# RMS normalisation: the inverse root mean square by an add and a power on GpSimd in place of Sqrt on ScalarE and a reciprocal on VectorE

## The chip, the cores and the metric

The kernel runs on one core of a Trainium2 chip. The metric is the device time of one execution in microseconds (us), the median over several executions. The engines are named as in the profile: PE (TensorE), DVE (VectorE), ACT (ScalarE), POOL (GpSimd) and SP (SyncE, which here only issues transfers). Each runs its own instructions in the order in which they were written and waits for others by semaphores.

## The reference

```python
batch, seq, dim = 16, 1024, 512          # x: 16 x 1024 x 512 float32, gamma: ones(512)

def reference(x, gamma):
    eps = 1e-5
    rms = np.sqrt(np.mean(x ** 2, axis=-1, keepdims=True) + eps)
    return (x / rms * gamma).astype(np.float32)
```

There are 16,384 rows of 512 numbers. Each row is divided by its own root mean square and multiplied by gamma, number by number. 33.55 MB are read and as many written.

## The kernel before

**Tiling.** The rows are cut into four tiles t = 0 to 3 of 128 partitions x 32 rows x 512 numbers (8.4 MB each). Three of them fit into the buffers `slot0` to `slot2`; tile 3 goes into slot 0 again, once tile 0 has been stored from there. Compute works in nine groups, `(t, g, n, pieces, share)` in the list `groups`: group (t, g) is the n rows per partition from row g of tile t. The first two groups have 7 and 9 rows, the other seven have 16.

**The work of a group.**
- `square_sums` (L88): for each piece of 7, 5 or 4 rows ACT squares into a scratch buffer (L92), DVE sums along the row into `ss` (L93). `ss` has one column per row of the group.
- `inverse_rms` (L97): ACT takes Sqrt(ss / 512 + eps) of all n columns (L98), DVE the reciprocal (L99). The result stands in `ss` and is called `rstd`.
- `scale_by_pool` (L102): POOL takes the last `share` rows (7 of 16, as a rule; 3 in the last group), multiplies them by `rstd` (L105) and then by gamma (L106), in place.
- `scale` (L111): ACT multiplies the other `mine` rows by `rstd`, one instruction per row (L114); `times_gamma` (L116): DVE multiplies them by gamma in one instruction (L118).

**The order** is written out by hand. Iteration k issues, for group k, `scale_by_pool`; the first two pieces of `square_sums` of group k + 1; the first half of `scale`; the third piece of k + 1; the second half of `scale`; `times_gamma`; the transfers; and at its very end `inverse_rms` of group k + 1. So before the change the Sqrt of group k + 1 stands behind the last L114 of group k on ACT, and its reciprocal behind L118 of group k on DVE. POOL's queue has L105 and L106 of each group and nothing else after the start.

**Transfers.** All are issued by SP, in one queue. `load` is at L45 and `store` at L49. The loads of tiles 0 and 1 are issued at the start and those of tile 2 after the first group, among three one-row stores. After group (0, 16) follow the stores of rows 3 to 15 and 16 to 31 of tile 0 and the two loads of tile 3; tiles 1 and 2 are stored whole, after groups (1, 16) and (2, 16), and tile 3 in halves, after (3, 0) and (3, 16). A store waits on SP for POOL's and DVE's products, and what follows it on SP waits too.

**Start.** Gamma arrives as one row; TensorE multiplies a column of ones with it (L66), which spreads it over 128 partitions of `gamma_psum`, and ACT copies that into `gamma_b` for POOL (L161). L72 is a Sqrt on one column of constants.

Of the kernel before, what the change touches and what calls it, by code (L numbers as in the profile page):

```python
# [9 lines left out]
def kernel(  # L10
# [6 lines left out]
    nc = tc.nc  # L17
    P = nc.NUM_PARTITIONS
    eps = 1e-5
    fp32 = mybir.dt.float32  # L20
    AF = mybir.ActivationFunctionType
    OP = mybir.AluOpType
# [3 lines left out]
    N, D = xf.shape  # L26
# [9 lines left out]
    const = ctx.enter_context(tc.tile_pool(name="const", bufs=1))  # L36
# [24 lines left out]
    load(1, 1, 16, 32)  # L61

    ones_col = const.tile([1, P], fp32)
    nc.gpsimd.memset(ones_col, 1.0)  # L64
    gamma_psum = psum.tile([P, 1, D], fp32, name="gamma_psum")
    nc.tensor.matmul(gamma_psum[:, 0], ones_col, gamma_row, start=True, stop=True)  # L66
    gamma_b = const.tile([P, 1, D], fp32)

    eps_t = const.tile([P, 1], fp32)
    nc.gpsimd.memset(eps_t, eps)  # L70
    table = const.tile([P, 1], fp32)
    nc.scalar.activation(out=table, in_=eps_t, func=AF.Sqrt)  # L72


    groups = [
# [19 lines left out]
        )  # L95

    def inverse_rms(ss, n):  # L97
        nc.scalar.activation(out=ss[:, :n, 0], in_=ss[:, :n, 0], func=AF.Sqrt, bias=eps_t, scale=1.0 / D)  # L98
        nc.vector.reciprocal(out=ss[:, :n, 0], in_=ss[:, :n, 0])  # L99
        return ss  # L100

    def scale_by_pool(rstd, t, g, n, share):  # L102
# [44 lines left out]
    def pieces_of(group):  # L147
        t, g, n, pieces, share = group
        ss = stats.tile([P, 16, 1], fp32, name="ss")
        r = 0  # L150
        todo = []
        for k, m in enumerate(pieces):
            todo.append((ss, t, g, r, m, k))
            r += m
        return ss, todo

    ss, todo = pieces_of(groups[0])
    for piece in todo:
        square_sums(*piece)
    rstd = inverse_rms(ss, groups[0][2])  # L160
    nc.scalar.copy(out=gamma_b[:, 0], in_=gamma_psum[:, 0])  # L161
    for k, group in enumerate(groups):
        t, g, n, pieces, share = group
        mine = n - share
        half = (mine + 1) // 2
        ahead = groups[k + 1 :][:1]
        ss, todo = pieces_of(ahead[0]) if ahead else (None, [])
        scale_by_pool(rstd, t, g, n, share)
        for piece in todo[:2]:
            square_sums(*piece)  # L170
        scale(rstd, t, g, 0, half)
        for piece in todo[2:]:
            square_sums(*piece)
        scale(rstd, t, g, half, mine)
        times_gamma(t, g, 0, mine)
        transfers(t, g)
        for nxt in ahead:
            rstd = inverse_rms(ss, nxt[2])
# [30 lines left out]
```

## Time and profile before

| | |
|---|---|
| median of 3 executions | 161.61 us (161.46 to 161.80) |
| the profiled execution | 161.56 us |
| its span in the profile | 159.5 us |
| DVE, ACT, POOL busy | 112.5, 108.2, 106.4 us (71%, 68%, 67%) |
| read and written | 33.56 and 33.55 MB, 421 GB/s over the span |

The span is what the profiler saw of the program on the core; the time of the execution has 2.06 us around it. A group of instructions is shown as line, engine, operation, output and inputs with their shapes, then the count, the busy time in all, the mean ns of one, and the idle time of the engine just before them with what ended it. The digits of a row of slices are tenths of a fortieth of the span. The transfers have a row of their own, since they run on DMA engines beside the five.

### The profile page before, as it was taken

Reading aid. Unit: us, or ns where it says so; the run is one execution under the profiler, and the core shown is the slowest. Engines: PE = TensorE matmul, PEld = TensorE weight load, DVE = VectorE, ACT = ScalarE, POOL = GpSimd, SP = SyncE. Lnnn points to the kernel's source line nnn. Section 1 sums busy time; section 2 is a strip of 40 time slices with the busy share of each in tenths; the row PEclk is TensorE's granted clock in tenths of the full one; section 3 lists DMA queues with packets and bytes.
Section 4 is the critical chain, followed back from the end, with each engine's and each line's share of the span. In section 5 each row is a group of like instructions: output and inputs, shape, how many; then the busy total and the mean of one; then the engine's idle time right before and its main releaser. Section 6 shows DMA issues by size and latency. Waiting matters only on the chain.

```text
span 159.5 us, 280 instructions
## 1 busy us (share of the span) xinstructions
PE 2.0 (1%) x2; PEld 0.5 (0%) x2; DVE 112.5 (71%) x42; ACT 108.2 (68%) x111; POOL 106.4 (67%) x24
## 2 busy tenths in 40 slices
PE   0050000000000000000000000000000000000000
PEld 0010000000000000000000000000000000000000
DVE  0028597997989999999999999899997019500000
ACT  3072989859999998998999499999942970000000
POOL 1000947986998699999999999999999940000000
DMA  5999999999999999999999999996996996999995
GB/s 199 424 431 493 427 394 419 501 394 394 460 394 396 454 415 419 427 452 403 509 403 394 501 419 394 526 526 263 526 493 296 526 493 296 394 435 485 394 403 255
DMA packets 2747, 67.12 MB, mean 421 GB/s; under 512 B 313, under 2 KB 314, under 8 KB 698
## 3 DMA queue, kind: packets, MB, share of 16 engines
q1 hardware_dynamic: 2746, 67.11, 98.2%
q14 instruction: 1, 0.01, 0.0%
HBM read 33.56 MB, written 33.55 MB: 421 GB/s over the span
## 4 chain that ended last, share of the span: by engine, by line
DMA 38%; DVE 29%; ACT 16%; issue 2%; ACTq 0%; SPq 0%
DMA out_dram<-slot 22%; DMA slot<-in_x_dram 17%; DVE ss L93 17%; DVE slot L118 12%; ACT slot L114 8%; ACT sq_psum L92 6%; ACT sq_sbuf L92 1%; ACTq L204 0%; ACT ss L98 0%; ACT gamma_b L161 0%; DVE ss L99 0%; SPq L49 0%; ACTq L92 0%
## 5 line engine op out<-in xcount | busy, mean ns | idle before, releaser
L105 POOL TENSOR_TENSOR slot<-slot,ss 128x3584 f32<-128x3584 f32 (+2 forms) x9 | 46.9, 5216 | 21.7 <-DVE ss L99 21.7
L93 DVE TENSOR_REDUCE ss<-sq_psum 128x7 f32<-128x3584 f32 (+1 forms) x16 | 49.2, 3073 | 16.5 <-ACT sq_psum L92 16.5
L106 POOL TENSOR_TENSOR slot<-slot,gamma_b 128x3584 f32<-128x3584 f32 (+2 forms) x9 | 59.2, 6582 | 0.7
L114 ACT ACTIVATE slot<-slot,ss 128x512 f32<-128x512 f32 x75 | 47.5, 709 | 4.7 <-DVE ss L99 4.7
L118 DVE TENSOR_TENSOR slot<-slot,gamma_psum 128x4608 f32<-128x4608 f32 (+2 forms) x9 | 41.3, 4592 | 8.5 <-ACT slot L114 8.5
L92 ACT ACTIVATE sq_psum<-slot 128x3584 f32<-128x3584 f32 (+1 forms) x16 | 40.2, 2512 | 8.4 <-DMA slot<-in_x_dram 7.0
L93 DVE TENSOR_REDUCE ss<-sq_sbuf 128x5 f32<-128x2560 f32 x8 | 22.5, 2808 | 0.0
L92 ACT ACTIVATE sq_sbuf<-slot 128x2560 f32<-128x2560 f32 x8 | 18.6, 2323 | 0.0
L98 ACT ACTIVATE ss<-ss,eps_t 128x16 f32<-128x16 f32 (+2 forms) x9 | 2.7, 304 | 8.4 <-DVE ss L93 8.4
L99 DVE RECIPROCAL ss<-ss 128x16 f32<-128x16 f32 (+2 forms) x9 | 2.1, 237 | 0.4 <-ACT ss L98 0.4
L66 PE MATMUL gamma_psum<-gamma_row,ones_col 1*128 1x512 f32 x2 | 2.0, 1120 | 8.6 <-DMA gamma_row<-in_gamma_dram 8.6
L72 ACT ACT_TABLE_LOAD x1 | 1.3, 1283 | 1.1 <-PEq L193 1.1
L161 ACT COPY gamma_b<-gamma_psum 128x512 f32<-128x512 f32 x1 | 0.6, 565 | 0.0
L66 PEld LDWEIGHTS gamma_psum<-gamma_row,ones_col 1*128 1x128 f32 x2 | 0.5, 304 | 8.6 <-issue 8.6
L64 POOL MEMSET ones_col<- 1x128 f32 x1 | 0.2, 195 | 0.3 <-POOLq L193 0.3
L193 POOL MEMSET const-float32-0.0<- 128x1 f32 x1 | 0.1, 99 | 0.2 <-issue 0.2
L72 ACT ACTIVATE table<-eps_t 128x1 f32<-128x1 f32 x1 | 0.2, 202 | 0.0
L193 POOL MEMSET const-bfloat16-1.0<- 128x1 bf16 x1 | 0.1, 103 | 0.0
L193 POOL MEMSET const-uint8-127<- 128x1 uint8 x1 | 0.1, 103 | 0.0
L193 POOL MEMSET const-float32-1.0<- 128x1 f32 x1 | 0.1, 99 | 0.0
L70 POOL MEMSET eps_t<- 128x1 f32 x1 | 0.1, 89 | 0.0
## 6 DMA issues: line engine op xcount, KB each, us to landing
slot<-in_x_dram SPq DMA_DIRECT2D x6, 4096.0 KB, 21.8
out_dram<-slot SPq DMA_DIRECT2D x3, 4096.0 KB, 23.3
slot<-in_x_dram SPq DMA_DIRECT2D x4, 2048.0 KB, 9.9
out_dram<-slot SPq DMA_DIRECT2D x1, 3328.0 KB, 34.5
out_dram<-slot SPq DMA_DIRECT2D x3, 256.0 KB, 31.9
gamma_row<-in_gamma_dram SPq DMA_DIRECT2D x4, 0.4 KB
out_dram<-slot SPq DMA_DIRECT2D x2
gamma_row<-in_gamma_dram SPq DMA_DIRECT2D x1, 0.5 KB
```

Of the source, the lines that this page charges most:

```text
L66: nc.tensor.matmul(gamma_psum[:, 0], ones_col, gamma_row, start=True, stop=True)
L72: nc.scalar.activation(out=table, in_=eps_t, func=AF.Sqrt)
L92: nc.scalar.activation(out=sq[:, :m], in_=rows, func=AF.Square)
L93: nc.vector.tensor_reduce(out=ss[:, r : r + m, 0], in_=sq[:, :m], axis=mybir.AxisListType.X, op=OP.add)
L98: nc.scalar.activation(out=ss[:, :n, 0], in_=ss[:, :n, 0], func=AF.Sqrt, bias=eps_t, scale=1.0 / D)
L99: nc.vector.reciprocal(out=ss[:, :n, 0], in_=ss[:, :n, 0])
L105: nc.gpsimd.tensor_tensor(out=part, in0=part, in1=by_row, op=OP.mult)
L106: last = nc.gpsimd.tensor_tensor(out=part, in0=part, in1=gamma_b.to_broadcast([P, share, D]), op=OP.mult)
L114: nc.scalar.activation(out=x[:, g + r, :], in_=x[:, g + r, :], func=AF.Copy, scale=rstd[:, r])
L118: scaled = nc.vector.tensor_tensor(out=part, in0=part, in1=gamma_psum.to_broadcast([P, r1 - r0, D]), op=OP.mult)
L161: nc.scalar.copy(out=gamma_b[:, 0], in_=gamma_psum[:, 0])
L193: nc = _bacc.Bacc("TRN2", target_bir_lowering=False, num_devices=1)
```

## The change

`inverse_rms` becomes two instructions on POOL: an add of 512 x eps to the sum of squares, and a power with the exponent -0.5, each with its second operand spread from one column. As the sum is not divided by 512 any more, gamma is multiplied by the square root of 512 where it is spread: the column of ones that TensorE multiplies with it becomes a column of that number. The Sqrt at L72 and its constants go; two other constant columns are written on POOL.

```diff
     ones_col = const.tile([1, P], fp32)
-    nc.gpsimd.memset(ones_col, 1.0)
+    nc.gpsimd.memset(ones_col, D**0.5)
...
-    eps_t = const.tile([P, 1], fp32)
-    nc.gpsimd.memset(eps_t, eps)
-    table = const.tile([P, 1], fp32)
-    nc.scalar.activation(out=table, in_=eps_t, func=AF.Sqrt)
+    eps_d = const.tile([P, 1, 1], fp32)
+    nc.gpsimd.memset(eps_d, eps * D)
+    power = const.tile([P, 1, 1], fp32)
+    nc.gpsimd.memset(power, -0.5)
...
     def inverse_rms(ss, n):
-        nc.scalar.activation(out=ss[:, :n, 0], in_=ss[:, :n, 0], func=AF.Sqrt, bias=eps_t, scale=1.0 / D)
-        nc.vector.reciprocal(out=ss[:, :n, 0], in_=ss[:, :n, 0])
+        nc.gpsimd.tensor_tensor(
+            out=ss[:, :n], in0=ss[:, :n], in1=eps_d.to_broadcast([P, n, 1]), op=OP.add
+        )
+        nc.gpsimd.tensor_tensor(
+            out=ss[:, :n], in0=ss[:, :n], in1=power.to_broadcast([P, n, 1]), op=OP.pow
+        )
         return ss
```

The place of `inverse_rms` in the order stays: at the end of iteration k, for group k + 1. On POOL that is behind L106 of group k.

## The prediction

> **What bounds the kernel now.** I read the page's 40 slices and queue table first, since 67 MB moved in 159.5 us suggests transfers. They say that the DMA engines never rest, from slice 2 to the end:
>
> ```profile
> DMA  5999999999999999999999999996996996999995
> q1 hardware_dynamic: 2746, 67.11, 98.2%
> ```
>
> The three 6s have to be checked, so next I cut the span into long stretches (columns: busy us and instructions of PE, its weight load, DVE, ACT and POOL, clock, DMA share, GB/s):
>
> ```profile
> 0.00:2.00 2.00, 0.00 (x0) 0.00 (x0) 0.00 (x0) 0.85 (x1) 0.44 (x6) 1.00 0.30 70
> 72.00:109.00 37.00, 0.00 (x0) 0.00 (x0) 36.10 (x15) 34.07 (x34) 36.77 (x6) 1.00 1.02 439
> 109.00:138.00 29.00, 0.00 (x0) 0.00 (x0) 20.80 (x7) 16.18 (x25) 20.20 (x5) 1.00 1.00 434
> 138.00:158.00 20.00, 0.00 (x0) 0.00 (x0) 0.00 (x0) 0.00 (x0) 0.00 (x0) 1.00 0.97 419
> ```
>
> The share is 1.00 and more from 72 to 138 us, where the 6s lie: a 6 is large packets falling into unequal slices, not a pause. So the transfers set the time, at about 433 GB/s, where a 4096 KB store (4.19 MB) is 9.7 us of data. In 72 to 109 us POOL is busy 36.77 of 37 us and DVE 36.10: the compute engines are full as well, but they run ahead of the transfers. By how much is read from issue and landing (last column: us from issue to landing) of the first load, issued at 0.74, and of the last two stores, issued at 123.16 and 138.0:
>
> ```profile
> slot<-in_x_dram SPq DMA_DIRECT2D x1, 2048.0 KB, 7.2
> out_dram<-slot SPq DMA_DIRECT2D x1, 4096.0 KB, 25.9
> out_dram<-slot SPq DMA_DIRECT2D x1, 4096.0 KB, 20.7
> ```
>
> The stores land at 149.1 and 158.7, 9.6 us apart: the last one only queued. On an empty queue the first load took 7.2 us, of which 2.10 MB / 433 GB/s = 4.8 is data and so 2.3 us other latency; the last store alone would take 9.7 + 2.3 = 12.0. To land at 158.7 it need only be issued at 146.7. **Compute has 8.7 us to spare** (146.7 - 138.0). The chain of waits stops at the last DVE instruction and does not show this.
>
> What sets the 138.0 is in the timeline (start, duration, engine, line):
>
> ```profile
> 109.11 6.17 POOL L105 TENSOR_TENSOR slot<-slot,ss 128x3584 f32<-128x3584 f32 x1
> ...
> 115.36 7.78 POOL L106 TENSOR_TENSOR slot<-slot,gamma_b 128x3584 f32<-128x3584 f32 x1
> ...
> 117.72 0.31 ACT L98 ACTIVATE ss<-ss,eps_t 128x16 f32<-128x16 f32 x1 [0.56 <-DVE ss L93]
> 122.46 0.25 DVE L99 RECIPROCAL ss<-ss 128x16 f32<-128x16 f32 x1
> 122.74 8.07 ACT L114 ACTIVATE slot<-slot,ss 128x512 f32<-128x512 f32 x13 [4.71 <-DVE ss L99]
> 123.09 2.75 POOL L105 TENSOR_TENSOR slot<-slot,ss 128x1536 f32<-128x1536 f32 x1
> ...
> 130.85 7.09 DVE L118 TENSOR_TENSOR slot<-slot,gamma_psum 128x6656 f32<-128x6656 f32 x1 [8.14 <-ACT slot L114]
> ```
>
> POOL starts its pair L105, L106 at 53.12, 67.11, 81.12, 95.10, 109.11 and 123.09: every 14.0 us, with no idle. From the last inverse root mean square (122.71) to the last store are 15.3 us: 8.1 on ACT, 7.1 on DVE, the rest waits.
>
> **What the Trainium skill says.** GPSIMD Engine Reference, 3.1 (side-by-side cycle accounting), gives about 2.6 cycles per element for a two-input elementwise instruction; Specifications gives 1.2 GHz. The trace agrees roughly, by the groups kept apart by shape:
>
> ```profile
> L106 POOL TENSOR_TENSOR slot<-slot,gamma_b 128x3584 f32<-128x3584 f32 x6 | 46.8, 7794 | 0.5
> L105 POOL TENSOR_TENSOR slot<-slot,ss 128x3584 f32<-128x3584 f32 x6 | 37.0, 6164 | 3.9 <-DVE ss L99 3.9
> ...
> L106 POOL TENSOR_TENSOR slot<-slot,gamma_b 128x1536 f32<-128x1536 f32 x2 | 6.9, 3437 | 0.2
> ...
> L105 POOL TENSOR_TENSOR slot<-slot,ss 128x1536 f32<-128x1536 f32 x2 | 5.5, 2751 | 14.7 <-DVE ss L99 14.7
> ```
>
> L105: (6164 - 2751) / 2048 = 1.67 ns, 2.0 cycles; L106: 2.13 ns, 2.6 cycles. Both leave 0.19 us fixed (2751 - 1536 x 1.667). The same page, 7 (performance pitfalls for Q7 kernels), gives 4 cycles for each step of a dependent fp32 chain. No page prices a power. Perfetto Trace Analysis, Tensor Engine Instruction, calls GPSIMD strict FIFO; here every POOL pair runs in program order.
>
> **The change part by part.** Removed: nine Sqrt on ACT (0.30 us) and nine reciprocals on DVE (0.25). That is worth nothing at the end: neither engine ends the kernel while transfers do, and both pace less tightly than POOL (reciprocals at 52.79, 66.48, 80.17: 13.7 us per group). It does bring squares forward by up to 0.5 us, where ACT stood waiting at L98.
>
> The table warm-up at L72 goes; a table load must then stand ahead of the first Square. I cost it at 0: the load takes 1.28 us (ScalarE: Activation LUTs, "What ACT_TABLE_LOAD costs", says about 1283 ns, as the trace does) and the first rows land at 7.9. Without that cover it would be 1.3 us once, early, inside POOL's idle of 3.2 us at 25 us. The memsets of other values cost the same; the second constant is some 0.1 us at 1 us, under the wait for data.
>
> Added: two POOL instructions per group, and a **new place in a queue**. The reciprocal of the next group stood behind L118 on DVE. The add and the power stand behind L106 of this group on POOL, and POOL has no idle there. Behind them wait L105 on POOL, L114 on ACT, L118 on DVE and the store on SP. So each group's period becomes 14.0 + q, with q the add, the power and gaps.
>
> - Add on 128x16: 0.19 + 16 x 1.67 ns = 0.22 us.
> - Gaps: 0.1 us for two more handovers (L105 ends 59.29, L106 starts 59.36: 0.07 each, rounded down).
> - Power on 128x16: unknown. The floor is an add, 0.22 us. The page's Specifications give eight cores with 16 fp32 lanes, so one column of 128 rows is one vector step, 16 per instruction. A power is a logarithm, a product and an exponential, which I take as some 20 to 40 dependent steps with range handling: at 4 cycles 80 to 160 cycles, or 0.07 to 0.13 us a column if columns don't overlap. Overlapped, it could be a third; done lane by lane, 16 times as much (some 20 to 30 us). I take **2.1 us** (0.19 + 16 x 0.12), in the upper half, since a generic loop with special cases seems likelier to me than a pipelined one.
>
> So q = 0.22 + 2.1 + 0.1 = 2.4 us for 16 columns. Sum over the path: the sums of squares of group (0, 16) are ready at 34.9, up to 0.5 sooner by the freed ACT; I take 34.5. POOL is free then: group (0, 7) can begin at 22.7, takes 1.6 for its nine columns and 10.1 for its pair, to 34.4. From there POOL is never idle again: seven q and six pairs of 14.0 to the last inverse root, 34.5 + 84 + 7 x 2.4 = 135.3. With the 15.3 behind it, the last store is issued at 150.6, 3.9 us beyond 146.7. It then starts on an empty queue and is late by all of that. The profiled execution took 161.56 us for a span of 159.5, that is 2.06 around it, and the median is 161.61: 161.6 + 3.9 = **165.5 us**.
>
> The same sum gives the threshold: 34.5 + 84 + 7q + 15.3 = 146.7 at q = 1.84, a power of 1.5 us. Below, nothing shows; above, each further us of power costs 7 us, and 9 once the two short groups queue too. Earlier stores don't decide: that of (2, 16) goes out at 104.5 + 5q and has 38.8 us of data and 3.1 of latency and close behind it, to 146.4 + 5q, less than the last store's 146.6 + 7q.
>
> **The rivals.**
> - **A, forecast: power of 1.5 to 3.5 us.** Ends 161.9 to 177 (3.5 us: the two short groups at q = 2.0 and 2.4, seven at 3.8; POOL from 15.05 on is 100.4 of pairs plus 31.0; 146.5 + 15.3 = 161.8 issue, 15.1 late).
> - **B, not slower: the transfers hide it.** One mechanism: the 8.7 us of room before the last store. It decides for q up to 1.84. POOL even starts ahead, because at 24.8 and 37.0 the inverse root no longer waits behind L118. Time 161.6. For it speaks that an overlapped vector loop needs under 1 us; against it, that seven groups each pay.
> - **C, the power is very slow (over 3.5 us)**, partly or wholly lane by lane. At 5 us: q of 5.3 (seven), 2.6 and 3.2 sum to 42.9; 15.05 + 100.4 + 42.9 + 15.3 = 173.7, plus 12.8 to the end of the span and 2.06: 188.5. At 20 us, over 300.
> - **D, faster**: ACT and DVE relieved. The engines that move data are busy 98.2% of the span, and the rest is the start and the last landing, which the change leaves alone. At most a few tenths: 161.2.
> - That the change doesn't do what it says, as by a table load that waits for data, comes out as B.
>
> **How the numbers follow.** Chances: A 0.40, B 0.37, C 0.18, D 0.05. About 0.2% (0.3 us) is what can be told from no change. A gives slower, C too: 0.58; B gives 0.37 within; D 0.05 faster. The range takes in B and A whole and C to a power of some 4.3 us (183): 161.2 to 183, leaving out some 0.12 of C and a little of D. A alone: 161.9 to 177.
>
> **What would show it.** After: add and power between L106 and the next L105; their mean is the whole question. POOL's pair would start every 14.0 + q from 37 us on. If q is above 1.84, the last store lands some 12 us after its issue and the DMA row has a real gap before it; if below, it lands later than that and the row stays full. I am wrong in mechanism if the DMA row has gaps earlier than the last stores, if POOL is idle between groups, or if L105 or L106 themselves change length.

## The result and the profile after

| | before | after |
|---|---|---|
| median of 4 executions | 161.71 us (161.46 to 163.47) | 171.82 us (171.66 to 171.92) |
| ratio to before | | 1.060, 95% interval 1.0525 to 1.0675 |
| profiled execution, its span | 161.56, 159.5 us | 171.83, 170.0 us |
| POOL, DVE, ACT busy | 106.4, 112.5, 108.2 us | 131.8, 112.0, 105.7 us |

The kernel is slower, as forecast, but by 10.1 us where 3.9 were forecast. The page of after, its DMA row, queue table and chain of waits:

```profile
DMA  5999999999898999999999999997559995950885
q1 hardware_dynamic: 2746, 67.11, 92.4%
POOL 73%; ACT 7%; DVE 6%; DMA 4%; issue 1%; ACTq 0%; POOLq 0%
```

The same 67.11 MB now fill 92.4% of a longer span, and the chain runs 73% over POOL. Before, it was made of DMA, DVE and ACT:

```profile
DMA 38%; DVE 29%; ACT 16%; issue 2%; ACTq 0%; SPq 0%
```

The 5s and the 0 late in the row of after have to be explained. After, cut into stretches around them (columns as before: PE, its weight load, DVE, ACT, POOL, clock, DMA share, GB/s):

```profile
109.00:118.00 9.00, 0.00 (x0) 0.00 (x0) 5.50 (x3) 9.00 (x10) 8.92 (x2) 1.00 1.07 466
118.00:122.00 4.00, 0.00 (x0) 0.00 (x0) 4.00 (x2) 2.69 (x2) 4.00 (x1) 1.00 0.00 0
122.00:151.00 29.00, 0.00 (x0) 0.00 (x0) 12.55 (x5) 15.49 (x23) 26.32 (x9) 1.00 1.01 434
151.00:158.00 7.00, 0.00 (x0) 0.00 (x0) 6.67 (x1) 0.00 (x0) 0.00 (x0) 1.00 0.00 0
158.00:168.00 10.00, 0.00 (x0) 0.00 (x0) 0.00 (x0) 0.00 (x0) 0.00 (x0) 1.00 0.98 419
```

These two are real pauses, but shorter than they look. A packet is booked where it starts, and the large ones take 2.4 us each, so a stretch can show 0.00 while packets that started before it still move. From the start and length of every packet in the trace, none is under way for 3.2 us (119.7 to 122.9) and for 6.4 us (152.2 to 158.6), 9.6 of the 10.5 us by which the span grew. Before, neither existed. The first ends when the store of tile 2 is issued (122.1), the second when the last store is (157.7). The groups of after, kept apart by shape, show what filled POOL:

```profile
L101 POOL TENSOR_TENSOR ss<-ss,power 128x16 f32<-128x16 f32 x7 | 20.3, 2906 | 0.5
...
L101 POOL TENSOR_TENSOR ss<-ss,power 128x9 f32<-128x9 f32 x1 | 1.8, 1797 | 0.1
L98 POOL TENSOR_TENSOR ss<-ss,eps_d 128x16 f32<-128x16 f32 x7 | 1.5, 218 | 0.0
L101 POOL TENSOR_TENSOR ss<-ss,power 128x7 f32<-128x7 f32 x1 | 1.5, 1488 | 0.1
```

The add costs 0.22 us as worked out; the power on 16 columns costs 2.91 us, not 2.1. From 7 to 16 columns it grows by (2906 - 1488) / 9 = 158 ns a column, and 0.38 us is fixed. The end of the timeline of after:

```profile
125.29 6.16 POOL L109 TENSOR_TENSOR slot<-slot,ss 128x3584 f32<-128x3584 f32 x1
...
131.53 7.77 POOL L110 TENSOR_TENSOR slot<-slot,gamma_b 128x3584 f32<-128x3584 f32 x1
...
139.26 0.21 POOL L98 TENSOR_TENSOR ss<-ss,eps_d 128x16 f32<-128x16 f32 x1
139.55 2.91 POOL L101 TENSOR_TENSOR ss<-ss,power 128x16 f32<-128x16 f32 x1
142.49 8.07 ACT L118 ACTIVATE slot<-slot,ss 128x512 f32<-128x512 f32 x13 [9.82 <-POOL ss L101]
...
150.59 7.09 DVE L122 TENSOR_TENSOR slot<-slot,gamma_psum 128x6656 f32<-128x6656 f32 x1 [12.93 <-ACT slot L118]
```

POOL runs L109, L110, add, power without a pause, every 17.27 us (108.01 to 125.29) where the pair alone took 14.0. ACT stands for 9.82 us until the last power is done at 142.46; before, the last reciprocal was done at 122.71. What lies behind it is as long as before (15.2 us to the issue), and the last store landed 11.1 us after its issue: it no longer queued.

### The profile page after: what moved, and what is told of

It reads as the page before. It is cut to its first block, busy times and chain, and to the rows that moved or that the text cites. A ratio compares the mean times of both kernels' runs of the same rounds, so it can differ in the third digit from the quotient of the medians.

```text
span 170.0 us, 290 instructions
## 1 busy us (share of the span) xinstructions
PE 2.0 (1%) x2; PEld 0.5 (0%) x2; DVE 112.0 (66%) x33; ACT 105.7 (62%) x101; POOL 131.8 (78%) x43
## 3 DMA queue, kind: packets, MB, share of 16 engines
q1 hardware_dynamic: 2746, 67.11, 92.4%
## 4 chain that ended last, share of the span: by engine, by line
POOL 73%; ACT 7%; DVE 6%; DMA 4%; issue 1%; ACTq 0%; POOLq 0%
POOL slot L110 33%; POOL slot L109 26%; POOL ss L101 13%; ACT slot L118 4%; DMA slot<-in_x_dram 4%; DVE slot L122 4%; ACT sq_psum L92 3%; DVE ss L93 2%; POOL ss L98 1%; ACTq L208 0%; POOLq L109 0%; POOLq L110 0%
## 5 line engine op out<-in xcount | busy, mean ns | idle before, releaser
L118 ACT ACTIVATE slot<-slot,ss 128x512 f32<-128x512 f32 x75 | 47.5, 707 | 31.4 <-POOL ss L101 31.4
L110 POOL TENSOR_TENSOR slot<-slot,gamma_b 128x3584 f32<-128x3584 f32 (+2 forms) x9 | 59.3, 6585 | 0.7
L92 ACT ACTIVATE sq_psum<-slot 128x3584 f32<-128x3584 f32 (+1 forms) x16 | 40.1, 2505 | 12.3 <-DMA slot<-in_x_dram 6.6
L109 POOL TENSOR_TENSOR slot<-slot,ss 128x3584 f32<-128x3584 f32 (+2 forms) x9 | 46.9, 5215 | 0.7
L101 POOL TENSOR_TENSOR ss<-ss,power 128x16 f32<-128x16 f32 (+2 forms) x9 | 23.6, 2626 | 0.7
L98 POOL TENSOR_TENSOR ss<-ss,eps_d 128x16 f32<-128x16 f32 (+2 forms) x9 | 1.9, 215 | 14.3 <-DVE ss L93 14.3
L72 POOL MEMSET power<- 128x1 f32 x1 | 0.1, 89 | 0.0
```

The lines of the kernel that those rows point to most:

```text
L92: nc.scalar.activation(out=sq[:, :m], in_=rows, func=AF.Square)
L98: nc.gpsimd.tensor_tensor(out=ss[:, :n], in0=ss[:, :n], in1=eps_d.to_broadcast([P, n, 1]), op=OP.add)
L101: nc.gpsimd.tensor_tensor(out=ss[:, :n], in0=ss[:, :n], in1=power.to_broadcast([P, n, 1]), op=OP.pow)
L109: nc.gpsimd.tensor_tensor(out=part, in0=part, in1=by_row, op=OP.mult)
L110: last = nc.gpsimd.tensor_tensor(out=part, in0=part, in1=gamma_b.to_broadcast([P, share, D]), op=OP.mult)
L118: nc.scalar.activation(out=x[:, g + r, :], in_=x[:, g + r, :], func=AF.Copy, scale=rstd[:, r])
```

## The experiments

The theory: POOL's queue sets the pace, because the power stands in it behind L110 with nothing idle; this delays the stores until the transfers run dry, and the last store most, as ACT and DVE do their 15.2 us behind the last power. The rivals: the place alone, or the handovers from POOL to ACT; POOL's busy time alone, wherever it is spent; the other edits (gamma's factor, constants, table).

**Another instruction in the same place (e1).**

```diff
-            out=ss[:, :n], in0=ss[:, :n], in1=power.to_broadcast([P, n, 1]), op=OP.pow
+            out=ss[:, :n], in0=ss[:, :n], in1=power.to_broadcast([P, n, 1]), op=OP.mult
```

> The changed kernel with a multiply in place of the power: same place in POOL's queue, same waits; the power itself is left out. Theory (the length of the power, paid once per group in POOL's queue): the 16-column instruction falls from 2.91 to about 0.22 us, the period of POOL from 17.27 to about 14.6, the last store is issued near 138 us, inside the room before the transfers: 161.6 us. Rival 1 (the place: ACT and DVE now wait for POOL at the end of each group, whatever the instruction takes): most of the 10 us stays, over 168. Rival 2 (the table warm-up or gamma's factor): stays at 171.8.

161.96 us, ratio 1.0006 (0.9995 to 1.0016). The group and the DMA row of e1:

```profile
L101 POOL TENSOR_TENSOR ss<-ss,power 128x16 f32<-128x16 f32 x7 | 1.5, 216 | 0.6
```
```profile
DMA  6999999999999999999999999996996996999993
```

With 0.22 us in the power's place the row has the same three 6s as before the change and no 5: the last store went out at 138.1 us, as it did before. The place, the waits and all other edits are still there, so none of them carries the loss by itself. The place is not free: POOL starts a group every 14.57 us (93.71 to 108.28) instead of 14.0. But its first large group starts 2.0 us sooner than before (35.41 for 37.36), since its inverse root no longer stands behind L118 on DVE, and so the last inverse root is done at 122.77, where it was done at 122.71 before.

**Half of the columns (e2).**

```diff
+        m = 8 if n == 16 else n
-            out=ss[:, :n], in0=ss[:, :n], in1=power.to_broadcast([P, n, 1]), op=OP.pow
+            out=ss[:, :m], in0=ss[:, :m], in1=power.to_broadcast([P, m, 1]), op=OP.pow
```

> The changed kernel with the power on 8 of the 16 columns in the seven large groups; for the other 8 the power is left out. By the three widths in the trace of after (7: 1.49, 9: 1.80, 16: 2.91 us) 8 columns take 1.65 us. Theory (period, then a threshold): period 16.0, last power ends at 35.6 + 6 x 16.0 + 1.95 = 133.6, last store issued at 148.9, about 2 us past the latest issue that the transfers hide (146.7 to 147.3): 163.2 to 163.8. Rival (every microsecond of the power counts, no room before the last store): 171.8 - 7 x 1.26 = 163.0, so this run alone doesn't tell it; with e1 at 161.6 and not at 153 it does.

162.50 us, ratio 1.0045 (1.0031 to 1.006): above before, and 0.7 us under the lower end of what was expected. The power and the last two stores of e2 (groups by shape; then issue and landing):

```profile
L102 POOL TENSOR_TENSOR ss<-ss,power 128x8 f32<-128x8 f32 x7 | 11.5, 1645 | 0.5
```
```profile
out_dram<-slot SPq DMA_DIRECT2D x1, 4096.0 KB, 18.1
```
```profile
out_dram<-slot SPq DMA_DIRECT2D x1, 4096.0 KB, 11.1
```

Eight columns took the 1.65 us of the straight line. The store before the last was issued at 131.2 and landed at 149.3; the last was issued at 148.4 and landed after 11.1, as on the empty queue of after. So this is the edge: the transfers had just about run dry (by the packets' times, for 0.2 us). It gives the room before the last store better than the first load did. From issue to the end of the span are 11.9 us (148.4 to 160.3), so the latest issue that costs nothing is 159.5 - 11.9 = 147.6, not 146.7, or 148.2 if the 0.2 us without a packet are taken off 148.4: the room is 9.6 to 10.2 us. e1 and e2 together show the threshold: from e1 to e2 the power grows by 1.43 us in each large group and the time by 0.5 us; from e2 to after it grows by 1.26 and the time by 9.3, that is 7.4 us for each microsecond. A little of this is the run's own: as L110's rows don't need the eight columns, POOL starts it without waiting for the power, and the period is 15.90 us, 0.1 less than was expected.

**Two powers (e3).**

```diff
+        nc.gpsimd.tensor_tensor(
+            out=spare[:, :n], in0=ss[:, :n], in1=power.to_broadcast([P, n, 1]), op=OP.pow
+        )
```

> The changed kernel with a second power per group on POOL, into spare columns, ahead of the one that counts. Theory (POOL is never idle from the first group on, so nine powers all show): 171.8 + 7 x 2.94 + 1.5 + 1.8 = 195.7 us. Rival (part of POOL's time is hidden by waits for ACT and DVE): less than 190.

195.68 us, ratio 1.2098 (1.208 to 1.2116). The nine extra powers (7 x 2.91, 1.79 and 1.49 us, 23.6 in all) show as 23.9 us: above the threshold nothing hides any of POOL's time.

**POOL as busy, but nobody waits (e4).**

```diff
+    def occupy_pool(n):
+        nc.gpsimd.tensor_tensor(out=spare[:, :n], in0=sums[:, :n], in1=power.to_broadcast([P, n, 1]), op=OP.add)
+        nc.gpsimd.tensor_tensor(out=spare[:, :n], in0=sums[:, :n], in1=power.to_broadcast([P, n, 1]), op=OP.pow)
...
         for nxt in ahead:
+            occupy_pool(nxt[2])
             rstd = inverse_rms(ss, nxt[2])
```

> The kernel before (Sqrt on ACT, reciprocal on DVE) with an add and a power per group on spare columns behind the multiply by gamma on POOL, which nobody waits for. POOL is as busy as after, but the inverse root doesn't come from it. Theory (two things add up: POOL's period delays every store, and the last group's 15.3 us of ACT and DVE stand behind the last power): only the first is left; the store of tile 2 goes out at about 121.3 instead of 109.2, some 4 us after the transfers ran dry, and the last one at about 148: 165.3 us. Rival 1 (POOL's busy time alone makes the loss): 171.8. Rival 2 (only the chain through the inverse root counts): 161.6.

164.54 us, ratio 1.0175 (1.0157 to 1.0193). POOL is busy for 129.9 us, 131.8 after (eight groups have the two instructions here, the first has none); the loss is 2.8 us of the 10.1. Both rivals fall. The time is 0.8 us under what was expected: the first pause had been put at some 4 us, and by the packets' times it is 2.3. Stretches of e4:

```profile
109.00:118.00 9.00, 0.00 (x0) 0.00 (x0) 9.00 (x5) 8.08 (x12) 8.92 (x2) 1.00 1.07 466
118.00:122.00 4.00, 0.00 (x0) 0.00 (x0) 4.00 (x1) 0.08 (x1) 3.92 (x3) 1.00 0.00 0
122.00:148.00 26.00, 0.00 (x0) 0.00 (x0) 7.85 (x3) 8.06 (x13) 25.55 (x7) 1.00 1.03 444
148.00:162.40 14.40, 0.00 (x0) 0.00 (x0) 0.00 (x0) 0.00 (x0) 0.00 (x0) 1.00 0.85 364
```

The first pause of after is here too, 118 to 122 us: the store of tile 2 waits for POOL's own rows and goes out at 121.3. The second is not: ACT starts the last group at 122.80, and the last store is issued at 147.8 onto a queue that still has work. So of the two pauses the first comes from POOL's rows being late, the second from the last inverse root being late.

**The last power earlier in the queue (e7).**

```diff
+        if early:                        # (t, g) == (3, 0)
+            following = inverse_rms(ss, ahead[0][2])
+            gamma_by_pool(part, t, g, n, share)
         scale(rstd, t, g, half, mine)
```

For this one group POOL's multiply by gamma (L110 after), here a function of its own, moves behind the add and the power of the last group.

> The changed kernel with the add and the power of the last group moved on POOL ahead of the multiply by gamma of the group before it; the other eight stay. Theory (queue position is what delays the last inverse root): the sums are ready at about 132.5, the power ends at about 135.8 instead of 142.5, the last store can be issued at 151 instead of 157.7. But the multiply by gamma of group (3, 0) ends at 143.6, so the store before the last goes out at 143.7 instead of 139.3, and the last queues behind it: data from 144.7 for 2 x 9.7 us, landing near 165, span about 166, 168 us. Rival 1 (only the last store's own issue counts): 151 + 12.1 + 1.8, 165. Rival 2 (order on POOL doesn't matter, its busy time does): 171.8.

167.33 us, ratio 1.0333 (1.029 to 1.0376). The end of the timeline of e7:

```profile
132.63 2.91 POOL L101 TENSOR_TENSOR ss<-ss,power 128x16 f32<-128x16 f32 x1
135.50 7.78 POOL L113 TENSOR_TENSOR slot<-slot,gamma_b 128x3584 f32<-128x3584 f32 x1
135.57 8.07 ACT L121 ACTIVATE slot<-slot,ss 128x512 f32<-128x512 f32 x13 [3.15 <-POOL ss L101]
143.23 2.76 POOL L109 TENSOR_TENSOR slot<-slot,ss 128x1536 f32<-128x1536 f32 x1
143.67 7.09 DVE L125 TENSOR_TENSOR slot<-slot,gamma_psum 128x6656 f32<-128x6656 f32 x1 [6.26 <-ACT slot L121]
```

ACT starts 6.9 us sooner (135.57 for 142.49) and the last store goes out at 150.8 instead of 157.7, but the time falls by only 4.5 us. The store before it now waits for L113 and goes out at 143.3 instead of 139.3; the last landed 13.3 us after its issue, behind it. The two issues came within 0.4 us of what was expected (143.7 and 151), and the time ended 0.7 us under the 168: position in the queue counts, and what is late next takes part of it back.

**Less of the other work on POOL (e5).**

```diff
-        (0, 16, 16, (7, 5, 4), 7),      # and five more groups
+        (0, 16, 16, (7, 5, 4), 6),
```

> The changed kernel with POOL's share cut from 7 to 6 of the 16 rows in the six groups that had 7; ACT and DVE take 10 instead of 9. Theory (POOL's period): the pair shrinks by 512 x (1.67 + 2.13) ns = 1.94 us, the period from 17.27 to 15.3, last power ends at 35.6 + 6 x 15.3 + 3.2 = 130.6, last store issued near 146, under the 147.6 that run e2 implies: 161.6 to 162. DVE's period rises to some 14.4, still under POOL's. Rival 1 (the price is the power's place: ACT waits for it, whoever does the rows): over 168. Rival 2 (DVE or ACT becomes the bound): last store after 148, 163 and more.

161.80 us, ratio 1.0005 (0.9986 to 1.0023). Groups of e5 and the start of its last group:

```profile
L110 POOL TENSOR_TENSOR slot<-slot,gamma_b 128x3072 f32<-128x3072 f32 x6 | 40.2, 6704 | 0.5
L122 DVE TENSOR_TENSOR slot<-slot,gamma_psum 128x5120 f32<-128x5120 f32 x6 | 32.9, 5487 | 4.2 <-ACT slot L118 4.0
L109 POOL TENSOR_TENSOR slot<-slot,ss 128x3072 f32<-128x3072 f32 x6 | 31.9, 5308 | 0.5
```
```profile
127.68 2.90 POOL L101 TENSOR_TENSOR ss<-ss,power 128x16 f32<-128x16 f32 x1
130.62 8.06 ACT L118 ACTIVATE slot<-slot,ss 128x512 f32<-128x512 f32 x13 [7.28 <-POOL ss L101]
```

One row fewer takes 1.9 us off POOL's pair. The last power ends at 130.6, the last store is issued at 145.9 and lands 13.0 later, so it queues again. The power is as long as after, in the same place, and POOL is still never idle between groups (every 15.3 us); yet the power costs nothing, since the last store again goes out before the latest issue. This repairs the changed kernel; it does not beat the one before, since both are held by the same transfers.

**Gamma's factor alone (e6).**

```diff
+        nc.scalar.activation(out=ss[:, :n, 0], in_=ss[:, :n, 0], func=AF.Sqrt, bias=eps_d[:, 0], scale=1.0)
+        nc.vector.reciprocal(out=ss[:, :n, 0], in_=ss[:, :n, 0])
```

The two POOL instructions of the changed kernel go; its factor on gamma stays.

> The changed kernel's gamma times sqrt(512) and constants, but with Sqrt on ACT (scale 1, bias 512 x eps) and the reciprocal on DVE, and the warm-up of the table as before. Theory (gamma's factor and the constants cost nothing): 161.6 us. Rival (part of the 10 us is the other scaling): above 162.

161.55 us, ratio 0.9983 (0.9966 to 1.0): no loss from the other scaling.

**Other exponents.** These were run once each, for the length of the instruction.

```diff
-    nc.gpsimd.memset(power, -0.5)
+    nc.gpsimd.memset(power, -1.0)      # 0.0 in the other
```

> The changed kernel with -1 as the exponent, so that the output is scaled by the inverse mean square and not by its root. If the price of the power is that of one general loop, the 16-column instruction stays at 2.91 us and the time at 171.8. If exponents are told apart, it is shorter, and each 0.1 us less takes 0.9 us off.

> The changed kernel with 0 as the exponent: every row is scaled by 1 times sqrt(512). One general loop: 2.91 us and 171.8. A short way for simple exponents: under 1 us and 161.8.

171.99 and 171.95 us. The groups by shape have, in both, the same line for 16 columns:

```profile
L101 POOL TENSOR_TENSOR ss<-ss,power 128x16 f32<-128x16 f32 x7 | 20.3, 2905 | 0.5
```

Of the exponents -0.5, -1 and 0 none is cheaper than another.

## Why the prediction was right in direction and wrong in size

- *Compute has 8.7 us to spare before the last store.* Right in kind: e1 and e5 lengthen POOL's period and stay at 161.8 to 162.0. In size it is 9.6 to 10.2 us (from e2); the 2.3 us of latency, taken from a load, was too much for a store.
- *Removed instructions are worth nothing; the table load and gamma's factor cost nothing.* e6 shows it for gamma. For the removed ones, the transfers already filled 98.2% of the span; e1, which keeps the removal, gained nothing. The table load stood ahead of the first Square at 1.14 us, under the wait for data, and took 1.28 us, as ScalarE: Activation LUTs, "What ACT_TABLE_LOAD costs", has it.
- *Each group's period becomes 14.0 + q.* Right: 17.27 us, without idle, so q is 3.27. Add and gaps were sized right (0.36 us together, against 0.32). POOL's own multiplies kept their length (L109 6.16, L110 7.80 us).
- *Power on 128x16: 2.1 us, 0.19 + 16 x 0.12.* **This is the term that failed.** It measured 2.91 us: 0.38 fixed and 0.158 a column. The prediction took the fixed part from the multiplies (0.19 from L105; L106 leaves 0.17) and the step from a count of dependent operations, with the 4 cycles each of GPSIMD Engine Reference, 7. At the 1.2 GHz that page gives, 158 ns are an estimated 190 cycles, above the 80 to 160 that were counted; no run here shows the clock, or what the engine does within a column, so whether the steps were too few or too cheap stays open. The real price lay inside the forecast's own case (1.5 to 3.5 us), but the point was put in it by guess, on a slope of 7 us for each microsecond.
- *POOL is free at 34.4, when the sums of (0, 16) are ready.* A smaller miss of the same kind: the powers on seven and nine columns took 1.49 and 1.80 us, where the same sizing gives 1.03 and 1.27, and the first add started 0.24 us later than the 15.05 assumed. So L110 of (0, 7) held POOL until 35.6.
- *34.5 + 84 + 7 x 2.4 = 135.3, then 15.3, then 12.8 and 2.06.* With the measured terms, 35.6 + 6 x 17.27 + 3.2 = 142.4, then 15.2, then 12.3 (157.7 to 170.0) and 1.83 gives 171.8. Of the 6.3 us that were missing, 6.0 are the longer q (5.7 of them the seven powers, 7 x 0.81), 1.1 the later start; the shorter end and the smaller time around the span take 0.8 back.
- *Earlier stores don't decide.* Right for the sum, since the last store goes out on an empty queue whatever came before. But the picture was incomplete: the store of tile 2 was late as well, and e4 shows that this would have cost 2.8 us by itself. The prediction had named a gap before the last stores as a sign that its mechanism is wrong, and the gap came. Its own terms give it, though: the end it worked out for that store, 146.4 + 5q, passes the 159.5 of before at q = 2.6, which the forecast of 2.4 had not reached and the measured 3.27 did. So the sign goes back to the size of the power, and was too strict.
- Of the rivals, that the transfers hide it holds nearly up to a power of 1.65 us on eight columns (e2, just over the edge) and fell at 2.91; lane by lane (20 us and more) and a gain did not come.

## What to carry to other kernels

Before moving a short operation to another engine, look at what stands ahead of it in that engine's queue and whether that queue ever idles: where it doesn't, the operation lengthens every round. Whether this costs time is a second question: here the same power cost 10 us, and nothing after 1.9 us of other work per group had left the queue, though that queue still had no idle. Where transfers set the time, compute has room up to a fixed latest issue of the last store, and behind it each microsecond per group counts once for every group; so with an unpriced operation ahead of such an edge, state the time as a function of the price rather than trust one value. When a late result is moved forward, price the next one that becomes late.

## What the runs showed of the hardware

- A power on POOL (fp32, the exponent spread from one column) costs 0.38 us and 158 ns for each column of 128 rows (7, 8, 9 and 16 columns: 1.49, 1.65, 1.80, 2.91 us), where an add on 16 columns costs 0.22 us. It does not depend on the exponent among -0.5, -1 and 0, nor on the data between sums of squares and a constant 512 (e4: 2.91 us).
- The first power of the kernel, on 7 columns, lies on the same line as the later ones, and a second power right behind one took 2.89 us (e3): no run shows a cost of first use.
- A store of 4096 KB on an empty or just emptying queue landed 11.1 us after its issue in four cases (after, e2, e3, e7), that is 1.4 us over its 9.7 us of data, and 11.8 us in a fifth (e3); the first load of the kernel had 2.3 us over its own.
